# Diagonal-matrix turns, five score banks and earlier value pages in a hybrid decoder step

## The chip, the cores and the metric

One NeuronCore of a Trainium2 chip runs the whole kernel as one program. The metric is the device time of one execution in microseconds; less is better. The engines named below are PE (TensorE; PEld is its weight load), DVE (VectorE), ACT (ScalarE), POOL (GpSimd) and SP (SyncE, which here only issues transfers).

## The reference

One inference step of four layers for a prompt of 1024 tokens and a sample group of 8 sequences with 4 new tokens each, all fp32. Layers 0 and 3 are short convolutions, layer 1 is an RG-LRU block, and layer 2, which the change is about, is differential attention with 8 heads (two score maps of 64 dimensions each, values of 128). The sample's past is 2048 tokens in pages of 128 rows, 16 pages for each sequence, found through a page table.

```python
def diff_combine(p, lam):
    p = p.reshape(p.shape[0], N_HEADS, 2, p.shape[2], p.shape[3])
    return p[:, :, 0] - lam * p[:, :, 1]

# prompt, one block of 128 queries at a time:
sc = jnp.einsum('bqhd,bkhd->bhqk', qi, k)
sc = jnp.where(kpos[None, :] <= qpos[:, None], sc, -jnp.inf)
w = diff_combine(jax.nn.softmax(sc, axis=-1), lam)
o = jnp.einsum('bhqk,bkhd->bqhd', w, v)
# sample: the same over k_past = cache_k[page_table], v_past = cache_v[page_table] and the new rows

def diff_attn_output(o, z, subln_g, lam_init, w_out):
    of = o * lax.rsqrt(jnp.mean(jnp.square(o), axis=-1, keepdims=True) + SUBLN_EPS)
    of = of * subln_g * (1.0 - lam_init)
    return (of.reshape(bsz, t, V_WIDTH) * jax.nn.silu(z)) @ w_out
```

## The kernel before

Tiles are built by Python generators; a scheduler then sets the order on each engine from the order of emission, priorities and its own estimate of times. Layer 2 is `attn_layer`. It runs four main streams one after the other, and lays a side stream into each with `merge(main, total, side, cost)`: every main step yields a number of cost units, and the side stream may spend `cost / total` units for each.

1. `qkv` (line 1099 and around it): queries, keys and values of all tokens, written to DRAM (`qkT`, `vd`). Beside it runs `sample_keys`: POOL issues the 256 half pages of `cache_k` (line 1388 in `page`), DVE transposes each (line 1476), bursts of small matmuls (line 1420) make the scores, then a softmax, and `turn` writes the weights to DRAM (`psd`, lines 1457 and 1458).
2. `zpath`: the gate, 8 heads by 3 chunks of columns, 24 chunks of 24 matmuls (line 127); ACT takes a tanh (line 1160), DVE finishes it (line 1165), and SP stores it to `zd` (line 1166). The tile `zt` has two buffers. The sample keys go on beside it: `shares` of 0.76 and 0.26 divide their cost between the two streams.
3. `heads`: for 8 heads and 8 query blocks each. `keys` and `queries` read a head's keys and queries from DRAM (each 64-row half into both halves of the partitions, by `twice`, line 1183) and split them into a high and a low part. `score` makes the two maps (line 1210) into the banks of `mm`; DVE takes the minimum and adds the mask (lines 1248 and 1250); `expo` takes the exponential on ACT (line 1262). `combine` adds the second map to the first with the factor `rr[:, 10]` on DVE (line 1284). `turn` transposes the sum on PE (line 1293), ACT copies it out (line 1295), `apply` multiplies it with V (line 1303), `finish` scales (line 1312) and squares with a sum (line 1314) on ACT. Three blocks are under way at a time: scores of one, turn and apply of the one before, `finish` of the one before that.
4. Beside the heads runs `sample_values`: SP issues the 128 pages of `cache_v`, 512 KB each, into five buffers (`n_vp`), four matmuls a page accumulate them (line 1524, `sacc`), DVE scales the four row groups out of the bank (line 1530), and `gather_o` transposes them (line 1553).

PSUM has eight banks: tags P (3), Q (1), R (3) and U (1). `deal` says which tags each kind of tile takes in turn. In the heads, scores take R, turns, `pv` and the output's transposes take Q and U, the sample accumulator and `gather_o` take P. While the sample keys run, four of the banks are theirs (`psw`).

SP's queue is in order: a value page that waits for a free buffer holds up whatever SP issues after it.

Of the kernel before, what the change touches and what calls it, by code (L numbers as in the profile page):

```python
# [10 lines left out]
F32 = mybir.dt.float32  # L11
# [35 lines left out]
class Trunk:  # L47
# [31 lines left out]
    def bank(self, kind, name):  # L79
        tag = next(self.deals[kind])  # L80
        pool = self.psb if tag in "PQ" else self.psum
        return pool.tile([128, 512], F32, tag=tag, bufs=self.BANKS[tag], name=name)
# [1061 lines left out]
    def zpath(self, u):  # L1144
        nc, a = self.nc, self.a
        wv = a["d_w_in"][0].rearrange("(k p) f -> p k f", p=128)

        def ld(h):
            c = 3 * D + 128 * h
            return self.load_w(wv[:, :, c : c + 128], f"wz{h}")  # L1150

        wt = ld(0)
        for h in range(KB):
            nxt = ld(h + 1) if h < KB - 1 else None
            for c in range(3):
                c0, n = CH[c]
                npr = min(n, T - c0)
                ps = self.gemm_chunk(wt, u, c, f"zz{h}_{c}")
                t = self.sm(f"zt{h}_{c}")
                nc.scalar.activation(t[:, :n], ps[:, :n], AF.Tanh, scale=0.5)  # L1160
                if npr < n:
                    nc.vector.scalar_tensor_tensor(
                        self.szs[:, h], t[:, npr:n], 1.0, ps[:, npr:n], ALU.add, ALU.mult
                    )
                nc.vector.scalar_tensor_tensor(t[:, :npr], t[:, :npr], 1.0, ps[:, :npr], ALU.add, ALU.mult)  # L1165
                nc.sync.dma_start(self.zd[h][:, c0 : c0 + npr], t[:, :npr])
                yield 10.2 * n
            wt = nxt


    def heads(self, y):
# [13 lines left out]

        def keys(h, g):
# [6 lines left out]
            t = twice(1, h, g)  # L1193
            cs = slice(512 * g, 512 * g + 512)
            nc.scalar.copy(ks[h][:, :, cs], t)
            for s, (own, oth) in enumerate(halves):
                lo = ks[h][oth, s, cs]
                nc.gpsimd.tensor_tensor(lo, t[oth, s], lo.bitcast(F32), ALU.subtract)
# [76 lines left out]
        def combine(x):  # L1275
            qb, P, rr = x["qb"], x["P"], x["rr"]
            N = (qb + 1) * 128
            if N > 512:
# [5 lines left out]
            chain(nc.vector.scalar_tensor_tensor(  # L1284
                P[0][:, :N], P[1][:, :N], rr[:, 10:11], P[0][:, :N], ALU.mult, ALU.add))

        def turn(x):
            h, qb, P = x["h"], x["qb"], x["P"]
            x["w"] = []
            for o, w in chunks(qb):  # L1290
                wp = self.tp(f"wtp{h}_{qb}_{o}")
                for j in range(0, w, 128):
                    nc.tensor.transpose(wp[:, j : j + 128], P[0][:, o + j : o + j + 128], ident)
# [12 lines left out]
        def finish(x):  # L1306
# [7 lines left out]
            nc.scalar.activation(sq, O[0][:, qj], AF.Square, accum_out=ss[0][:, qj : qj + 1])  # L1314
# [16 lines left out]
        for nxt in blocks[1:] + [None, None, None]:  # L1331
# [24 lines left out]
            if old:  # L1356
                turn(old)
                yield 110 * (old["qb"] + 1)
# [36 lines left out]
    def sample_keys(self):  # L1395
# [95 lines left out]
        ck.__exit__(None, None, None)  # L1491
        self.cpb, self.psb = self.pool("psb2", space=PSUM, reuse_waits="tile")

# [55 lines left out]
    def gather_o(self, b, os_):  # L1549
        nc = self.nc  # L1550
        tp = self.tps(f"sot{b}")
# [9 lines left out]
    def attn_layer(self, l, u):  # L1561
# [30 lines left out]
        merge(itertools.islice(z, 20), ztot, keys, self.shares[1] * KEY_COST)  # L1592

        cpa, self.ppa = self.pool("ppa", reuse_waits="tile")
        hs = self.heads(u)
        next(hs)
        merge(z, ztot, keys, self.shares[1] * KEY_COST)
        rest(keys)
        ca, self.pp = self.pool("pp", reuse_waits="tile")
        self.deal(tp="QU", tps="P", mm="R")  # L1600
        tot = 64 * 9 * 110.0 + 288 * 324.0 + 16 * 430
        values = self.sample_values(u)
        next(values)
# [9 lines left out]
        merge(main(), tot, values, VALUE_COST * self.ahead)  # L1613
# [5 lines left out]
    def run(self):  # L1619
# [108 lines left out]
        if self.layers > 2:  # L1728
# [4 lines left out]
            self.shares, self.ahead, self.n_vp = (0.76, 0.26), 1.1, 5  # L1733
# [5 lines left out]
            for cm in (cr, cc, cs):  # L1739
                cm.__exit__(None, None, None)  # L1740
            trunk_bufs()
# [98 lines left out]
```

## Time and profile before

| | us |
|---|---|
| median of 3 runs | 2407.99 |
| lowest, highest | 2405.65, 2415.18 |
| the profiled execution | 2409.33 |
| its span | 2407.7 |

A row of the profile's tables by stage gives, for a window in us from the span's start, each engine's busy time with the number of instructions, the granted TensorE clock as a share of its full speed, the mean busy share of the 16 DMA engines, and what they moved. PE's busy time is modelled from overlapping matmuls, so the time between two starts in the timeline is the better measure of what an instruction costs. A row of waits names who waited, for whom, how long in total, how often, and the longest. The names are the program's tile names: `wtp` the turned P in PSUM, `wt` its copy, `pv` the product with V, `S` scores, `sacc` the sample accumulator, `vp` a value page, `kp` a key page.

### The profile page before, as it was taken

The page shows a single profiled execution, that of the slowest core. Times are in us where ns is not written, and L with a number is a line of the kernel's source. Part 1 is how long each engine was busy: PE and PEld are TensorE (multiplying, and loading weights), DVE is VectorE, ACT ScalarE, POOL GpSimd, SP SyncE. Part 2 cuts the span into 40 slices and gives each one's busy share as a digit, 9 for nine tenths or more (in the row PEclk, how much of TensorE's full clock was granted, in tenths as well). Part 3 has the DMA queues.
Part 4 walks back from the last instruction along what each step waited for, and adds up shares of the span by engine and source line. Part 5 has one row for each costly group of instructions (what it writes and reads, how often), then busy time and mean ns, then how long its engine had stood idle before and what let it go on. Part 6 is the DMA issues. An engine that isn't in the chain of part 4 may idle for free.

```text
span 2407.7 us, 45325 instructions
## 1 busy us (share of the span) xinstructions
PE 2277.3 (95%) x17288; PEld 1946.8 (81%) x17288; DVE 1453.2 (60%) x3015; ACT 929.2 (39%) x1906; POOL 337.1 (14%) x541
## 2 busy tenths in 40 slices
PE   7999999999999999988999998888888999999997
PEld 4989999997888886766666886555557999999997
DVE  6865655457456545656555554677675477666555
ACT  4333333346544423322221113667665243333410
POOL 0200000001001000233223322333220000000000
PEclk9999999999999999999999998999999999999999
DMA  9243344423444535768677766999993222222442
GB/s 329 77 145 111 91 121 150 133 82 120 139 131 124 154 108 171 217 201 255 222 242 253 244 189 203 277 298 291 281 299 116 84 85 62 68 59 70 128 131 76
DMA packets 289391, 393.41 MB, mean 163 GB/s; under 512 B 18749, under 2 KB 197054, under 8 KB 289174
## 3 DMA queue, kind: packets, MB, share of 16 engines
q1 hardware_dynamic: 247190, 306.61, 42.1%
q0 software_dynamic: 20480, 67.13, 9.1%
q10 hardware_dynamic: 21504, 16.78, 2.1%
q8 instruction: 136, 2.23, 0.4%
q14 instruction: 81, 0.66, 0.1%
HBM read 331.14 MB, written 59.31 MB: 162 GB/s over the span
## 4 chain that ended last, share of the span: by engine, by line
PE 64%; issue 13%; DMA 11%; POOLq 5%; POOL 2%; DVE 2%; ACT 1%; SPq 1%; DVEq 0%; ACTq 0%
PE op L127 15%; PE inX L612 12%; PE inZ L612 6%; DMA vp<-cache_v 6%; PE xb L127 4%; PE z L127 4%; POOLq L1381 4%; PE in L127 3%; PE inY L612 3%; PE ada L200 3%; PE in L733 2%; PE in L648 2%; PE g L903 2%; POOL kp L1388 2%; PE sacc L1524 1%
## 5 line engine op out<-in xcount | busy, mean ns | idle before, releaser
L1099 PE MATMUL qk<-wq,ua 128*128 128x512 f32 x1152 | 284.1, 401 | 8.7 <-DVE wq L1067 5.5
L1099 PEld LDWEIGHTS qk<-wq,ua 128*128 128x128 f32 x1152 | 213.2, 189 | 68.4 <-DVE wq L1067 8.1
L1476 DVE STREAM_TRANSPOSE kt<-kp 128x512 f32<-128x512 f32 x256 | 172.0, 697 | 138.5 <-DMA kp<-cache_k 107.1
L1388 POOL DMA_DIRECT2D kp<-cache_k x256 | 137.9, 539 | 336.1 <-DVE kt L1476 188.8
L294 DVE SCALAR_TENSOR_TENSOR r<-op,gate,xr 128x384 f32<-128x384 f32 (+1 forms) x96 | 54.2, 570 | 127.4 <-PE op L127 82.5
L1262 ACT ACTIVATE P<-S,rr 128x512 f32<-128x512 f32 (+2 forms) x192 | 110.8, 583 | 47.1 <-DVE rr L1250 31.5
L1210 PE MATMUL S<-ks,qhl 128*128 128x512 f32 (+2 forms) x384 | 110.8, 395 | 13.8 <-ACT P L1262 7.4
L127 PE MATMUL zz<-ua,wz 128*128 128x384 f32 (+1 forms) x576 | 99.0, 331 | 7.0 <-DVE zt L1165 7.0
L1210 PEld LDWEIGHTS S<-ks,qhl 128*128 128x128 f32 x384 | 60.8, 196 | 54.8 <-ACT P L1262 30.7
L127 PEld LDWEIGHTS zz<-ua,wz 128*128 128x128 f32 x576 | 95.6, 193 | 11.4 <-DVE zt L1165 7.8
L127 PEld LDWEIGHTS z<-ub,wrz 128*128 128x128 f32 x576 | 92.6, 188 | 11.7 <-issue 10.1
L1524 PE MATMUL sacc<-vp,pv 128*16 128x256 f32 x1024 | 80.3, 389 | 22.9 <-DMA vp<-cache_v 22.7
L127 PE MATMUL z<-ub,wrz 128*128 128x384 f32 (+1 forms) x576 | 98.2, 326 | 0.0
L1303 PEld LDWEIGHTS pv<-V,wt 128*128 128x128 f32 x576 | 73.7, 194 | 22.5 <-ACT wt L1295 13.4
L127 PEld LDWEIGHTS xb<-ub,wrx 128*128 128x128 f32 x504 | 80.9, 188 | 12.7 <-issue 9.2
L1420 PE MATMUL sps<-kt,qbd 32*32 32x512 f32 x2048 | 78.8, 621 | 11.9 <-DVE kt L1476 11.9
L331 POOL TENSOR_TENSOR rs<-mv,mhalf 128x1 f32<-128x1 f32 (+1 forms) x36 | 19.1, 541 | 504.3 <-DVE mv L329 497.6
L127 PE MATMUL op<-ua,ub 128*128 128x384 f32 (+1 forms) x504 | 89.7, 333 | 0.0
L127 PEld LDWEIGHTS op<-ua,ub 128*128 128x128 f32 x504 | 81.9, 192 | 9.1 <-issue 9.0
L127 PE MATMUL xb<-ub,wrx 128*128 128x384 f32 (+1 forms) x504 | 87.9, 328 | 0.0
L1303 PE MATMUL pv<-V,wt 128*128 128x128 f32 x576 | 82.3, 284 | 5.8 <-ACT wt L1295 5.3
L200 PE MATMUL ada<-wada,ct 128*32 128x512 f32 x384 | 82.7, 616 | 4.1 <-DMA wada<-w_ada 2.9
(492 smaller groups left out, 5112.4 us busy)
## 6 DMA issues: line engine op xcount, KB each, us to landing
kp<-cache_k POOLq DMA_DIRECT2D x256, 256.0 KB, 3.8
vp<-cache_v SPq DMA_DIRECT2D x128, 512.0 KB, 10.0
wada<-w_ada SPq DMA_DIRECT2D x96, 512.0 KB, 4.2
xa<-xat SPq DMA_DIRECT2D x64, 192.0 KB, 2.6
wra<-a_w_in SPq DMA_DIRECT2D x24, 512.0 KB, 4.1
wrb<-a_w_in SPq DMA_DIRECT2D x24, 512.0 KB, 4.1
xr<-xa SPq DMA_DIRECT2D x64, 192.0 KB, 2.5
tok<-kd SPq DMA_DIRECT2D x32, 256.0 KB, 7.0
```

The costliest lines, as they stand in the source:

```text
L127: nc.tensor.matmul(ps[:, :n], wt[:, wp, k], self.ucols(units[k], up, c), start=i == 0, stop=i == 3 * KB - 1)
L200: nc.tensor.matmul(ps[c : c + 32, :], self.ct[:, k], wts[k // 2][:, k % 2], start=k < 4, stop=k >= 4, tile_position=(0, c),)
L612: nc.tensor.matmul(B[tgt][jj][:, :QH], w[n][:, wp, k], mov[k](jj, up), start=new and m == 0, stop=m == 11, skip_group_check=not new)
L1099: nc.tensor.matmul(ps, u[k][:, c0 : c0 + 128], wq[n, k // 2][:, wp, k % 2], start=i == 0, stop=i == 3 * KB - 1)
L1210: nc.tensor.matmul(st[:, o : o + w], qs[h, g][:, part, s, 128 * qj : 128 * qj + 128], ks[h][:, s, l0 : l0 + w], start=part == 0, stop=part ...
L1262: nc.scalar.activation(p[:, o : o + w], x["S"][s][i][:, :w], AF.Exp, scale=-1.0, bias=rr[:, 6 + s : 7 + s], accum_out=rr[:, c : c + 1])
L1303: nc.tensor.matmul(x["pv"], x["w"][kb // 4][:, j : j + 128], V[h][:, kb], start=kb == 0, stop=kb == qb)
L1381: ld, (r,) = nc.values_load_multi_w_load_instructions(self.ptab[0:1, idx : idx + 1], engines=[et], min_val=0, max_val=159)
L1388: d = eng.dma_start(t, a[src].rearrange(pat)[bass.ds(r, 1), :, cs].rearrange("a p f -> p (a f)"))
L1420: nc.tensor.matmul(ps[b][32 * g : 32 * g + 32, r], qf[rows, f, g, k], kt[rows, g, k], start=f == 0 and k == 0, stop=f == 1 and k == 3, til ...
L1476: nc.vector.transpose(ktv[:, :, j], ring.pop(0).rearrange("p (f t) -> p f t", t=32))
L1524: nc.tensor.matmul(acc[32 * g : 32 * g + 16, :], pt[:k, j, g], vv[:k, :, g], start=j == 0, stop=j == NPG, tile_position=(0, 32 * g))
```

## The change

- `combine` no longer adds the two maps. It makes a 128 x 128 matrix `d` with the factor on its diagonal (DVE). `turn` makes, for each block of 128 columns, two matmuls that accumulate in PSUM: P0 with the identity and P1 with `d`.
- The square and its sum in `finish` move from ACT to DVE.
- PSUM after the sample keys: P has one bank, a new tag V has two. Scores take R, R, R, V, V in turn. `gather_o` takes Q and U in place of P. After layer 2 the pool is opened anew with three P banks.
- `keys` reads each key block once into a [128, 512] tile; ACT copies and POOL subtracts half by half.
- The sample keys must end after 12 of the 24 gate chunks (`shares` 0.8 and 0.4, and `rest(keys)` there). The sample values begin there, at 0.34 of their cost over the whole gate path, and the heads take the rest. `n_vp` is 7.
- In `zpath` the store to `zd` is issued by ACT, one chunk later, behind the next chunk's tanh.
- The pacing of the turns doubles, from 110 to 220 units for each block of 128.

```diff
--- before.py
+++ after.py
@@ -78,7 +78,7 @@
 
     def bank(self, kind, name):
         tag = next(self.deals[kind])
-        pool = self.psb if tag in "PQ" else self.psum
+        pool = self.psb if tag in "PQV" else self.psum
         return pool.tile([128, 512], F32, tag=tag, bufs=self.BANKS[tag], name=name)
 
     def tp(self, name):
@@ -1150,6 +1150,7 @@
             return self.load_w(wv[:, :, c : c + 128], f"wz{h}")
 
         wt = ld(0)
+        late = []
         for h in range(KB):
             nxt = ld(h + 1) if h < KB - 1 else None
             for c in range(3):
@@ -1158,14 +1159,17 @@
                 ps = self.gemm_chunk(wt, u, c, f"zz{h}_{c}")
                 t = self.sm(f"zt{h}_{c}")
                 nc.scalar.activation(t[:, :n], ps[:, :n], AF.Tanh, scale=0.5)
+                if late:
+                    nc.scalar.dma_start(*late.pop())
                 if npr < n:
                     nc.vector.scalar_tensor_tensor(
                         self.szs[:, h], t[:, npr:n], 1.0, ps[:, npr:n], ALU.add, ALU.mult
                     )
                 nc.vector.scalar_tensor_tensor(t[:, :npr], t[:, :npr], 1.0, ps[:, :npr], ALU.add, ALU.mult)
-                nc.sync.dma_start(self.zd[h][:, c0 : c0 + npr], t[:, :npr])
+                late.append((self.zd[h][:, c0 : c0 + npr], t[:, :npr]))
                 yield 10.2 * n
             wt = nxt
+        nc.scalar.dma_start(*late.pop())
 
 
     def heads(self, y):
@@ -1182,6 +1186,7 @@
             for rows in halves[0]:
                 nc.sync.dma_start(t[rows], src.rearrange("(s p) f -> p s f", p=64))
             return t
+
 
         def keys(h, g):
             if g == 0:
@@ -1190,12 +1195,13 @@
                 nc.sync.dma_start(
                     V[h], self.vd[:, 128 * h : 128 * h + 128].rearrange("(j p) f -> p j f", p=128)
                 )
-            t = twice(1, h, g)
+            t = self.raw([128, 512], f"tok1{h}_{g}")
             cs = slice(512 * g, 512 * g + 512)
-            nc.scalar.copy(ks[h][:, :, cs], t)
+            nc.sync.dma_start(t, self.qkT[1][128 * h : 128 * h + 128, cs])
             for s, (own, oth) in enumerate(halves):
-                lo = ks[h][oth, s, cs]
-                nc.gpsimd.tensor_tensor(lo, t[oth, s], lo.bitcast(F32), ALU.subtract)
+                hi = ks[h][own, s, cs]
+                nc.scalar.copy(hi, t[own])
+                nc.gpsimd.tensor_tensor(ks[h][oth, s, cs], t[own], hi.bitcast(F32), ALU.subtract)
 
         def queries(h, g):
             t = twice(0, h, g)
@@ -1273,16 +1279,17 @@
             last.append(inst)
 
         def combine(x):
-            qb, P, rr = x["qb"], x["P"], x["rr"]
-            N = (qb + 1) * 128
-            if N > 512:
+            qb, rr = x["qb"], x["rr"]
+            if qb > 3:
                 chain(nc.vector.tensor_reduce(
                     rr[:, 0:2], rr[:, 16:20].rearrange("p (s i) -> p s i", s=2), axis=AX.X, op=ALU.add))
             chain(nc.vector.reciprocal(rr[:, 4:6], rr[:, 0:2]))
             chain(nc.vector.scalar_tensor_tensor(
                 rr[:, 10:11], rr[:, 0:1], rr[:, 5:6], self.nlam, ALU.mult, ALU.mult))
-            chain(nc.vector.scalar_tensor_tensor(
-                P[0][:, :N], P[1][:, :N], rr[:, 10:11], P[0][:, :N], ALU.mult, ALU.add))
+            x["d"] = d = self.ropep.tile([128, 128], F32, tag="dg", bufs=2, name=f"dg{x['h']}_{qb}")
+            chain(nc.vector.tensor_scalar(d, ident, rr[:, 10:11], None, ALU.mult))
+
+
 
         def turn(x):
             h, qb, P = x["h"], x["qb"], x["P"]
@@ -1290,7 +1297,9 @@
             for o, w in chunks(qb):
                 wp = self.tp(f"wtp{h}_{qb}_{o}")
                 for j in range(0, w, 128):
-                    nc.tensor.transpose(wp[:, j : j + 128], P[0][:, o + j : o + j + 128], ident)
+                    for s, r in enumerate((ident, x["d"])):
+                        nc.tensor.matmul(
+                            wp[:, j : j + 128], P[s][:, o + j : o + j + 128], r, start=s == 0, stop=s == 1)
                 wt = self.pp.tile([128, 512], F32, tag="wt", bufs=self.n_wt, name=f"wt{h}_{qb}_{o}")
                 nc.scalar.copy(wt[:, :w], wp[:, :w])
                 x["w"].append(wt)
@@ -1311,7 +1320,9 @@
                 ss[0] = self.ropep.tile([128, 4], F32, tag="ss", bufs=2, name=f"ss{h}_{g}")
             nc.scalar.activation(O[0][:, qj], x["pv"], AF.Identity, scale=x["rr"][:, 4:5])
             sq = self.ropep.tile([128, 128], F32, tag="sq", bufs=1, name=f"sq{h}_{qb}")
-            nc.scalar.activation(sq, O[0][:, qj], AF.Square, accum_out=ss[0][:, qj : qj + 1])
+            nc.vector.tensor_tensor_reduce(
+                sq, O[0][:, qj], O[0][:, qj], scale=1.0, scalar=0.0, op0=ALU.mult, op1=ALU.add,
+                accum_out=ss[0][:, qj : qj + 1])
 
         def begin(h, qb):
             return dict(h=h, qb=qb, S={}, P=[], rr=self.ropep.tile(
@@ -1355,7 +1366,7 @@
                     out.append((older["h"], older["qb"] // 4, outputs(older["h"], older["qb"] // 4)))
             if old:
                 turn(old)
-                yield 110 * (old["qb"] + 1)
+                yield 220 * (old["qb"] + 1)
                 apply(old)
                 yield 216 * (old["qb"] + 1)
             if cur:
@@ -1489,7 +1500,9 @@
         turn(todo.pop())
         cw.__exit__(None, None, None)
         ck.__exit__(None, None, None)
+        self.BANKS = dict(self.BANKS, P=1, V=2)
         self.cpb, self.psb = self.pool("psb2", space=PSUM, reuse_waits="tile")
+        self.deal(tp="QU", tps="P", mm="RRRVV")
 
 
     def sample_values(self, y):
@@ -1548,7 +1561,7 @@
 
     def gather_o(self, b, os_):
         nc = self.nc
-        tp = self.tps(f"sot{b}")
+        tp = self.tp(f"sot{b}")
         for e in range(2):
             nc.tensor.transpose(tp[:, 128 * e : 128 * e + 128], os_[:, 128 * e : 128 * e + 128], self.ident)
         ov = self.ots[:, :, NQ * b : NQ * b + NQ].rearrange("p (e g) m -> p g e m", e=2)
@@ -1589,18 +1602,18 @@
         cq.__exit__(None, None, None)
         ct, self.tmp = self.pool("tmpq", reuse_waits="tile")
         z, ztot = self.zpath(u), 8 * 10.2 * NT
-        merge(itertools.islice(z, 20), ztot, keys, self.shares[1] * KEY_COST)
-
+        merge(itertools.islice(z, 12), ztot, keys, self.shares[1] * KEY_COST)
+        rest(keys)
+
+        values = self.sample_values(u)
+        next(values)
+        merge(itertools.islice(z, 8), ztot, values, self.zshare * VALUE_COST)
         cpa, self.ppa = self.pool("ppa", reuse_waits="tile")
         hs = self.heads(u)
         next(hs)
-        merge(z, ztot, keys, self.shares[1] * KEY_COST)
-        rest(keys)
+        merge(z, ztot, values, self.zshare * VALUE_COST)
         ca, self.pp = self.pool("pp", reuse_waits="tile")
-        self.deal(tp="QU", tps="P", mm="R")
-        tot = 64 * 9 * 110.0 + 288 * 324.0 + 16 * 430
-        values = self.sample_values(u)
-        next(values)
+        tot = 64 * 9 * 110.0 + 288 * 434.0 + 16 * 430
 
         def main():
             while True:
@@ -1610,7 +1623,7 @@
                     break
                 yield c
 
-        merge(main(), tot, values, VALUE_COST * self.ahead)
+        merge(main(), tot, values, VALUE_COST * (1 - self.zshare / 2) * self.ahead)
         rest(values)
         ca.__exit__(None, None, None)
         cpa.__exit__(None, None, None)
@@ -1730,14 +1743,16 @@
                 cm.__exit__(None, None, None)
             self.bufs = dict(sm=2)
             self.n_sz, self.n_ks, self.n_p, self.n_tok, self.n_wt, self.n_o = 1, 2, 4, 2, 3, 2
-            self.shares, self.ahead, self.n_vp = (0.76, 0.26), 1.1, 5
+            self.shares, self.zshare, self.ahead, self.n_vp = (0.8, 0.4), 0.34, 1.1, 7
             cc, cp = self.pool("acst", reuse_waits="tile", side="right")
             cr, self.ropep = self.pool("ropep", reuse_waits="tile", side="right")
             self.attn_consts(cp)
 
             self.attn_layer(2, A)
-            for cm in (cr, cc, cs):
+            for cm in (cr, cc, cs, self.cpb):
                 cm.__exit__(None, None, None)
+            self.BANKS = dict(self.BANKS, P=3)
+            self.cpb, self.psb = self.pool("psb3", space=PSUM, reuse_waits="tile")
             trunk_bufs()
             ca, self.tmpa = self.pool("tmp1a", reuse_waits="tile")
             cms, B = [ca], []
```

## Rows read from the trace of the kernel before

**Rows 1.** The page's first line.

```profile
span 2407.7 us, 45325 instructions
```

**Rows 2.** Table by stage; columns: window, length, busy of each engine, PEclk, DMA share, GB/s.

```profile
948.00:1350.00 402.00, 375.12 (x3349) 270.37 (x3350) 221.92 (x459) 97.10 (x152) 112.52 (x209) 0.98 0.73 229
1350.00:1418.00 68.00, 61.97 (x636) 55.45 (x636) 40.51 (x79) 13.18 (x23) 20.62 (x39) 0.96 0.75 238
1418.00:1490.00 72.00, 63.03 (x638) 57.27 (x636) 27.40 (x48) 15.98 (x25) 20.59 (x25) 0.94 0.54 154
1490.00:1846.00 356.00, 304.39 (x2464) 200.09 (x2464) 252.52 (x658) 237.03 (x727) 100.53 (x72) 0.97 0.94 270
```

**Rows 3.** Transfers, 1490 to 1846 us: totals, then issues with count, size, median landing.

```profile
DMA packets 41000, 95.99 MB, mean 270 GB/s; under 512 B 3910, under 2 KB 14822, under 8 KB 40960
...
tok<-kd SPq DMA_DIRECT2D x24, 256.0 KB, 7.4
sz<-zd SPq DMA_DIRECT2D x15, 256.0 KB, 7.2
```

**Rows 4.** Groups by line and form, PE, 1490 to 1846: busy, mean ns, idle before.

```profile
L1303 PE MATMUL pv<-V,wt 128*128 128x128 f32 x576 | 82.3, 284 | 5.8 <-ACT wt L1295 5.3 <-ACT O L1312 0.5
L1524 PE MATMUL sacc<-vp,pv 128*16 128x256 f32 x1024 | 80.3, 389 | 22.9 <-DMA vp<-cache_v 22.7
L1210 PE MATMUL S<-ks,qhl 128*128 128x512 f32 x192 | 67.4, 443 | 4.1 <-ACT P L1262 4.0
L1293 PE MATMUL wtp<-ident,P 128*128 128x128 f32 x288 | 46.5, 285 | 8.0 <-DVE P L1284 7.5 <-ACT wt L1295 0.3
L1210 PE MATMUL S<-ks,qhl 128*128 128x256 f32 x124 | 28.4, 324 | 7.8 <-DVE zt L1165 5.9 <-ACT P L1262 1.6
L1210 PE MATMUL S<-ks,qhl 128*128 128x384 f32 x64 | 19.1, 396 | 1.9 <-ACT P L1262 1.8
```

**Rows 5.** Timeline of PE in the heads; columns: start us, length us, group.

```profile
1649.60 0.82 PE L1293 MATMUL wtp<-ident,P 128*128 128x128 f32 x6
1650.34 0.63 PE L1524 MATMUL sacc<-vp,pv 128*16 128x256 f32 x8
1650.90 1.60 PE L1303 MATMUL pv<-V,wt 128*128 128x128 f32 x12
1652.34 0.60 PE L1226 MATMUL ytp<-ident,O 128*128 128x128 f32 x4
...
1657.08 0.96 PE L1210 MATMUL S<-ks,qhl 128*128 128x512 f32 x4
1657.97 0.62 PE L1524 MATMUL sacc<-vp,pv 128*16 128x256 f32 x8
```

**Rows 6.** Waits, 1490 to 1846: engine, line, releaser, total us, times, longest.

```profile
PEld sacc L1524 <- DMA vp<-cache_v: 33.4, 34, 2.3
PEld S L1210 <- ACT P L1262: 30.7, 46, 6.1
...
PEld pv L1303 <- ACT wt L1295: 13.4, 24, 1.3
...
PE wtp L1293 <- DVE P L1284: 7.5, 8, 1.8
```

**Rows 7.** Timeline of POOL, gate path: issues of key pages.

```profile
1446.86 0.54 POOL L1388 DMA_DIRECT2D kp<-cache_k  x1 [0.82 <-issue]
1448.22 0.54 POOL L1388 DMA_DIRECT2D kp<-cache_k  x1 [0.82 <-DVE kt L1476]
```

**Rows 8.** Groups by line, DVE, 1490 to 1846: eviction of the sample accumulator.

```profile
L1530 DVE TENSOR_SCALAR os<-sacc,coef 16x256 f32<-16x256 f32 x32 | 15.4, 480 | 4.1 <-PE sacc L1524 3.6
```

**Rows 9.** Table by stage for 6.8 us of half clock, and PE's timeline there.

```profile
1515.60:1522.40 6.80, 6.18 (x30) 3.31 (x24) 3.06 (x6) 2.46 (x9) 0.00 (x0) 0.50 1.03 308
...
1515.47 1.03 PE L1524 MATMUL sacc<-vp,pv 128*16 128x256 f32 x8 [0.52 <-DMA vp<-cache_v]
```

**Rows 10.** Transfers of line 1166, the gate stores, over the span.

```profile
DMA to landing us min/median/max: 1.7/2.8/4.3
```

## The prediction

> **What bounds the kernel now.** The profiled execution took 2409.3 us, its span 2407.7 us [rows 1]; the median of the three timed runs, 2407.99 us, lies 1.3 us under that execution, and I bring the sum back by that at the end. The first view to read is the table by stage [rows 2]. The change touches four stretches: the projections with the sample keys beside them (948 to 1350 us), the first and second half of the gate path (1350 to 1418 and 1418 to 1490) and the prompt heads with the sample values beside them (1490 to 1846). In the heads no compute engine is full by its own column: PE is busy 304 of 356 us, DVE 253, ACT 237. The DMA share is 0.94, at 270 GB/s. In the second half of the gate path it is only 0.54. The reader should see that the heads hang on transfers, and that the stretch right before them has room for transfers.
>
> The next view, the transfers of the heads [rows 3], says what fills them: 96 MB, of which the 128 value pages of 512 KB (8 batches of 16) are 67 MB. The third view is PE's own work there [rows 4], priced not by busy time (matmuls overlap, and the mean of 284 ns is no pace) but by start to start in the timeline [rows 5]:
> - turning P: 288 instructions; six take 1650.34 - 1649.60 = 0.74 us, 0.123 each, together 36 us.
> - pv: 576 instructions for the 288 products of 128 x 128 (8 heads of 1 + 2 + ... + 8 blocks), so two instructions a product. Twelve take 1652.34 - 1650.90 = 1.44 us, 0.120 each, together 69 us.
> - sacc: eight, one page, take 0.56 us; 136 pages (128 and the 8 new rows, the last left out of the rows shown) make 76 us.
> - scores: four of 512 columns take 0.89 us, 0.2225 each; by columns 192 x 0.2225 + 64 x 0.167 + 124 x 0.111 = 67 us.
> Together 248 us. The other 108 us of the stage are small groups and waiting. The waits that PE's weight loads and matmuls show there [rows 6] are 33.4 us for value pages, 30.7 for score banks (ACT must read one out first), 13.4 for the turned P and 7.5 for the combined P: 85 us. So the stage has 85 us to give, and 23 us that I leave alone.
>
> **The change, part by part.**
> *Turns by a diagonal matrix.* A turn was one PE transpose of P, already combined by DVE. Now every 128 x 128 block takes two true products, P0 by the identity and P1 by the diagonal, added in PSUM. Operands are full fp32 and of the shapes of pv, and pv takes two instructions a product [rows 4]. So 288 instructions become 288 x 2 x 2 = 1152, 864 more. A wait-free pv instruction takes 0.120 us with its share of the change of group [rows 5]; the added ones only make groups longer, so I take somewhat less, 0.1125, an estimate: 864 x 0.1125 = **+97 us** on PE. Bounds: 0.10 to 0.12, so 86 to 104 us. The kernel's own pacing figures double the turn from 110 to 220 ns a block; the rows of pv say 450.
>
> What DVE is spared (the combination of up to 1024 columns, 64 times) and what it is given (a 128 x 128 diagonal and the square with its sum, taken from ACT) lie on engines with 100 us of slack [rows 2]: I cost them at nothing. If DVE were nearly full they would show as waits for the diagonal; the 7.5 us for the combined P fall to about 3, the chain being shorter.
>
> *Five banks for scores.* PE may run two more score tiles ahead of ACT. Of the 30.7 us I leave 9: scores also hang on the softmax's own order, which more banks don't change. Bounds 0 and 25 left.
>
> *Keys read once.* Each key half is read once instead of twice: of the 256 KB reads `tok<-kd` [rows 3] half go, 24 x 0.26 / 2 = 3.1 MB, 11 us of transfer at the stage's 270 GB/s. ACT copies two 64-partition halves instead of one 128-partition tile; hidden.
>
> *Values begin half way through the gate path.* 0.34 x 12/24 = 0.17 of the values' cost is spent there: 0.17 x 8 x 6900 = 9384 units, 400 a page and 500 a batch, about 22 pages. That takes 22 x 0.56 = **12 us** of PE and 11.5 MB out of the heads. The heads then carry 96 - 3.1 - 11.5 = 81 MB, at 270 GB/s 300 us of transfer, well under the PE work; with seven buffers instead of five the 33.4 us for pages fall to about 8 (bounds 2 and 20). The wait for the turned P falls from 13.4 to 9: longer turns hide the first chunk's copy.
>
> Relief in the heads: 85 - (8 + 9 + 9 + 3) = 56 us. **Heads: +97 - 12 - 56 = +29 us.** What is late next is PE itself: 248 + 97 - 12 = 333 us of work in a stage of 385.
>
> *Gate path.* The second half gains the 12 us of sacc; PE was idle there for 72 - 63 = 9 us [rows 2], and I let it absorb 4: +8 (bounds 0 and 14). Keys must now end after 12 chunks: 0.20 x 256 = 51 half pages in that half. POOL issues one every 1448.22 - 1446.86 = 1.36 us at its fastest [rows 7], so 70 us, as long as the whole half (68 us). The score bursts only move (their share of PE before 1350 rises from 0.76 to 0.80 and the gate path loses as much); I add 3 us for waiting on the last pages and the last turn (bounds -5 and +15). The gate stores leave SP, where they would queue ahead of value pages, for ACT's queue, and are issued one chunk later: 24 issues on an engine busy 29 us of 140, cost nothing while they land in time (third rival). **Gate path and keys: +11 us.**
>
> *One bank instead of three for the sample accumulator.* The first sacc of a batch now waits for four evictions of the last, 480 ns each [rows 8], and everything of PE behind it: at most 8 x 1.9 = 15 us, but main work of some microseconds is laid between two batches; I take 0. The pool that swaps these banks back before the last layers costs nothing: it closes when the heads have ended.
>
> Sum: 29 + 11 = +40 us, 2449 us in the profiled execution's terms, **2448 us** as a median.
>
> **A rule against the trace: the clock.** In the heads PE's granted clock averages 0.97; it is at 0.50, 1.2 of 2.4 GHz, from 1515.6 to 1522.4 us among others [rows 9], a stretch of 30 PE instructions whose sacc waits for pages [rows 9]. The Trainium skill, "TensorE: Matmul & The Clock Gate", Part 4 (PE-mode transpose), says that transposes don't count as PE activity for the clock as matmuls do. By it the new turns would hold the clock up by themselves and be worth up to 0.03 x 356 = 10 us, an estimate: 2438 us. The trace puts the drop behind late pages, not behind turns, and I leave the sum.
>
> **The rivals.**
> 1. *Waiting is all that grows less, and all of it goes.* If the whole 85 us vanish and the gate path absorbs its 12, the heads come out at +97 - 12 - 85 = 0 and the total at about 2408 us. For it: more banks, more buffers and a shorter chain all at once. Against: a PE at 333 us of work still has softmax chains between blocks, and PE-bound stretches of this kernel have gaps, as 948 to 1350 with 27 us idle [rows 2]. Chance 0.14, ends 2396 to 2420.
> 2. *The products cost what the pacing says.* If a product with the identity or the diagonal is one instruction like a transpose, the turns add only 288 x 0.1125 = 32 us. The heads then sit on the transfers' 300 us and PE's 268, and the relief outweighs the turns: 32 - 12 - 50 = -30, with +11 for the gate path -19 in all: 2389 us, **faster**. It decides from the instruction count: under about 600 in the turns. Against it: pv has the same types and shape and has two. Chance 0.06.
> 3. *The late store paces the gate path.* A gate tile has two buffers; its store is issued after the next chunk's tanh and must land before the one after that. The chunk can't be shorter than about 0.9 us (tanh and issue) plus the landing. Landing was 1.7 to 4.3 us, median 2.8 [rows 10], and a chunk with its share of pages lasts some 5.2 us, so it decides from a landing of 4.3 us. Beside value pages a read of like size took 7.2 us [rows 3]: 12 x (8.1 - 5.2) = +35, 2483 us. For it: the same wait is there before. Against: ACT's queue is not the pages' queue. Chance 0.13.
>
> **How the numbers follow.** Forecast 0.67 (own range 2420 to 2475), rivals 0.14, 0.06 and 0.13. The bounds of the terms reach from about 2408 (all relief) to about 2488 (25 us of relief, 20 in the gate path). With rival 1 half inside and rival 3 just inside, the range is 2408 to 2484. What a measurement of this kernel can tell from no change is about 0.5%, 12 us, so 2396 to 2420: faster 0.07 (rival 2 and the edge of rival 1), same 0.14 (rival 1 and the forecast's low edge), slower 0.79.
>
> **What would show it.** Turns of 1152 instructions at 0.11 to 0.12 us start to start prove the main term; 576 would prove rival 2. A stage of heads near 385 us with a DMA share near 0.75 and waits for value pages under 15 us would bear out that PE replaced the transfers as the bound; pages still late by 30 us would say that the move of 22 pages was not what they lacked. Waits of ACT for `zd` above 40 us would be rival 3. It goes wrong above all if PE's other waits, which I leave at 29 us, don't behave like a PE-bound stage's.

## The result and the profile after

| | before | changed |
|---|---|---|
| median, us | 2411.31 | 2470.37 |
| lowest, highest | 2405.65, 2415.18 | 2462.66, 2473.45 |
| the profiled execution | 2409.33 | 2470.98 |

The changed kernel takes 1.0242 of the time of before (95% interval 1.0208 to 1.0276): 59 us more. The forecast was 2448, the range 2408 to 2484, the likeliest side "slower". The profiled executions differ by 61.7 us, which I follow here.

Where it lies is read first from two tiles whose first and last matmul bound the heads: the scores `S` begin them, the turned outputs `ytp` end them. The view is that of one tile; columns are count, duration min/median/max in ns, first and last start in us. The kernel before:

```profile
L1210 PE MATMUL S<-ks,qhl x384: 274/392/796, 1482.8 to 1825.8; 128*128 128x512 f32 x96, 128*128 128x256 f32 x64, 128*128 128x384 f32 x32
L1226 PE MATMUL ytp<-ident,O x64: 272/273/421, 1523.4 to 1845.6; 128*128 128x128 f32 x64
```

The changed kernel:

```profile
L1216 PE MATMUL S<-ks,qhl x384: 274/392/505, 1507.4 to 1881.5; 128*128 128x512 f32 x97, 128*128 128x256 f32 x63, 128*128 128x384 f32 x32
L1232 PE MATMUL ytp<-ident,O x64: 270/273/328, 1550.9 to 1907.0; 128*128 128x128 f32 x64
```

The heads begin 1507.4 - 1482.8 = 25 us later and last 1907.0 - 1507.4 = 400 us in place of 1845.6 - 1482.8 = 363: 37 us more. The prediction had +11 and +29.

The table by stage of the changed kernel (columns as in [rows 2]); the heads are cut where the last value page is used:

```profile
948.00:1362.00 414.00, 383.63 (x3365) 272.13 (x3366) 229.12 (x477) 99.43 (x156) 119.87 (x219) 0.96 0.73 229
1362.00:1507.00 145.00, 135.12 (x1398) 109.79 (x1397) 60.53 (x111) 24.97 (x43) 31.58 (x51) 0.95 0.81 261
1507.00:1755.00 248.00, 241.98 (x2157) 172.05 (x2154) 136.26 (x459) 129.05 (x355) 67.64 (x48) 1.00 0.85 282
1755.00:1907.00 152.00, 138.86 (x1033) 126.18 (x1032) 89.13 (x321) 94.22 (x263) 37.10 (x27) 1.00 0.20 58
```

PE is busy 381 of the 400 us of the heads, against 304 of 356 before [rows 2]. The transfers are at 0.85 of their engines until 1755 us and at 0.20 after it. So the stage falls in two: a part with all 108 remaining pages, and 152 us after the last of them, in which PE is still busy 139 us and the transfers have little left.

The groups by line and the waits (columns as in [rows 4] and [rows 6]) for the heads of the changed kernel:

```profile
L1301 PE MATMUL wtp<-ident,P 128*128 128x128 f32 x576 | 113.3, 278 | 0.2 <-ACT O L1321 0.2
L1301 PE MATMUL wtp<-dg,P 128*128 128x128 f32 x576 | 111.5, 275 | 0.0
L1537 PE MATMUL sacc<-vp,pv 128*16 128x256 f32 x868 | 71.0, 383 | 2.8 <-DMA vp<-cache_v 2.8
```

```profile
PEld S L1216 <- ACT P L1268: 27.8, 53, 1.3
...
PE S L1216 <- ACT P L1268: 12.0, 24, 1.1
...
PEld sacc L1537 <- DMA vp<-cache_v: 6.9, 11, 1.4
...
PEld pv L1312 <- ACT wt L1304: 2.2, 7, 0.4
```

The turns are 576 + 576 = 1152 instructions, where there were 288 [rows 4]. No row of waits names the diagonal matrix. The timeline of PE, an unbroken stretch of them:

```profile
1606.44 0.39 PE L1301 MATMUL wtp<-dg,P 128*128 128x128 f32 x2
1606.66 0.39 PE L1301 MATMUL wtp<-ident,P 128*128 128x128 f32 x2
...
1607.78 0.39 PE L1301 MATMUL wtp<-dg,P 128*128 128x128 f32 x2
```

From 1606.44 to 1607.78 us lie 12 instructions: 0.112 us each. 864 more of them are 96 us of PE.

### The profile page after: what moved, and what is told of

Its sections match the earlier page's. It is cut to its first block, busy times and chain, and to the rows that moved or that the text cites. A ratio compares the mean times of both kernels' runs of the same rounds, so it can differ in the third digit from the quotient of the medians.

```text
span 2469.3 us, 47162 instructions
## 1 busy us (share of the span) xinstructions
PE 2372.9 (96%) x18152; PEld 2044.0 (83%) x18152; DVE 1426.7 (58%) x3143; ACT 913.0 (37%) x1794; POOL 340.5 (14%) x541
## 3 DMA queue, kind: packets, MB, share of 16 engines
q1 hardware_dynamic: 241430, 298.22, 37.9%
## 4 chain that ended last, share of the span: by engine, by line
PE 71%; issue 14%; POOLq 5%; DMA 4%; POOL 2%; ACT 1%; DVE 1%; SPq 0%; DVEq 0%; ACTq 0%
PE op L127 15%; PE inX L612 11%; PE inZ L612 6%; PE xb L127 4%; POOLq L1392 4%; PE z L127 4%; PE wtp L1301 4%; PE in L127 3%; PE inY L612 3%; PE sacc L1537 3%; PE ada L200 3%; PE S L1216 3%; PE zz L127 2%; PE in L733 2%; PE pv L1312 2%
## 5 line engine op out<-in xcount | busy, mean ns | idle before, releaser
L1301 PE MATMUL wtp<-ident,P 128*128 128x128 f32 x576 | 113.3, 278 | 0.2 <-ACT O L1321 0.2
L1301 PE MATMUL wtp<-dg,P 128*128 128x128 f32 x576 | 111.5, 275 | 0.0
L1431 PE MATMUL sps<-kt,qbd 32*32 32x512 f32 x2048 | 86.0, 682 | 17.2 <-DVE kt L1487 17.2
L1301 PEld LDWEIGHTS wtp<-ident,P 128*128 128x128 f32 x576 | 88.6, 191 | 9.7 <-issue 4.7
L1216 PEld LDWEIGHTS S<-ks,qhl 128*128 128x128 f32 x384 | 58.8, 189 | 40.0 <-ACT P L1268 27.8
L1301 PEld LDWEIGHTS wtp<-dg,P 128*128 128x128 f32 x576 | 87.4, 192 | 0.4 <-issue 0.4
```

The costliest lines, as they stand in the source:

```text
L1216: nc.tensor.matmul(st[:, o : o + w], qs[h, g][:, part, s, 128 * qj : 128 * qj + 128], ks[h][:, s, l0 : l0 + w], start=part == 0, stop=part ...
L1301: nc.tensor.matmul(wp[:, j : j + 128], P[s][:, o + j : o + j + 128], r, start=s == 0, stop=s == 1)
L1431: nc.tensor.matmul(ps[b][32 * g : 32 * g + 32, r], qf[rows, f, g, k], kt[rows, g, k], start=f == 0 and k == 0, stop=f == 1 and k == 3, til ...
```

## Experiments

Each kernel below was timed in three rounds against the kernel before, on one chip for each group; the kernel before stood at 2410 to 2411 us in all of them. "The changed kernel" stands at 2470.37 us.

### Old turns, all else changed

```diff
-                    for s, r in enumerate((ident, x["d"])):
-                        nc.tensor.matmul(
-                            wp[:, j : j + 128], P[s][:, o + j : o + j + 128], r, start=s == 0, stop=s == 1)
+                    nc.tensor.transpose(wp[:, j : j + 128], P[0][:, o + j : o + j + 128], ident)
```

with `combine` and the pacing as before the change.

> The changed kernel with the old turns: DVE combines the two maps and PE transposes the sum, 288 instructions instead of 1152; pacing as before; all else as changed. Theory (PE's work sets the end of the heads): 864 instructions at 0.112 us, 97 us of PE, go; transfers then limit the stage again at about 81 MB / 0.285 = 285 us, so the heads fall from 400 us to 300 to 325 and the kernel to about 2380 (2370 to 2400). Rival (the turns lie beside other waits and the loss comes from the new order and the moved keys): above 2430.

2381.53 us, 0.9894 of before (0.9869 to 0.9918): the turns cost the changed kernel 89 us, and what is left of the change gains 28 us. The first theory holds in that PE's work sets the end of the heads. The heads by stage:

```profile
1501.00:1816.00 315.00, 289.83 (x2319) 196.28 (x2318) 273.23 (x780) 218.49 (x616) 110.50 (x75) 0.98 0.78 249
```

315 us in place of 400, with PE busy 290 in place of 381. The theory's second half, that transfers limit the stage again, is not shown: the DMA share is 0.78.

### New turns alone

The same edit, the other way round, on the kernel before: the new turns and their pacing alone.

> The kernel before with the diagonal-matrix turns and their pacing alone. Theory: 97 us of PE come in, of which the waits for value pages (33 us) and for the turned and combined P (21 us) can hide some 45: about 2460 (2445 to 2480), value-page waits under 15 us. Rival (transfers stay the bound of the heads and hide the turns): within 12 us of before.

2490.27 us, 1.0347 (1.0309 to 1.0384): 80 us more than before, outside the 2445 to 2480 expected. The theory has the side right, its cover wrong: of the 97 us counted only some 17 were hidden, not 45. The stages, and the wait for pages from 1510 to 1850 us, say why:

```profile
1485.00:1808.00 323.00, 301.52 (x2566) 207.93 (x2568) 149.65 (x455) 166.30 (x493) 80.14 (x58) 0.98 0.93 282
1808.00:1923.00 115.00, 106.23 (x794) 97.38 (x793) 70.20 (x204) 77.41 (x238) 24.91 (x19) 0.99 0.19 55
...
PEld sacc L1525 <- DMA vp<-cache_v: 21.1, 20, 3.8
```

Up to the last page, at 1808 us, the transfers are at 0.93 and pages still come late; then 115 us follow with the transfers at 0.19. The cover that I counted on was there only in the first part, and the pages end long before the stage does.

### One product of the two

```diff
-                    for s, r in enumerate((ident, x["d"])):
-                        nc.tensor.matmul(
-                            wp[:, j : j + 128], P[s][:, o + j : o + j + 128], r, start=s == 0, stop=s == 1)
+                    nc.tensor.matmul(
+                        wp[:, j : j + 128], P[1][:, o + j : o + j + 128], x["d"], start=True, stop=True)
```

> The changed kernel with one of the two products of each turn (P1 by the diagonal; P0 by the identity is left out, so the attention of the first map is missing): 576 instructions fewer. Theory (PE-bound): 576 x 0.112 = 65 us less, 2400 to 2415. Rival (the heads wait for something else as soon as PE has a little room): less than 40 us gained, above 2430.

2398.62 us, 0.9955 (0.9937 to 0.9972): 72 us less than the changed kernel, for 576 instructions, or 0.125 us each. That is the full price of PE's time (0.112 us each) and a little more: the heads of the changed kernel are bound by PE.

### Three score banks, new turns

```diff
-        self.BANKS = dict(self.BANKS, P=1, V=2)
+        self.BANKS = dict(self.BANKS, P=3)
-        self.deal(tp="QU", tps="P", mm="RRRVV")
+        self.deal(tp="QU", tps="P", mm="R")
```

and `gather_o` back on P.

> The changed kernel with the banks dealt as before: three for scores (R), three for the sample accumulator and its transposes (P). The prediction's theory: five banks saved some 20 us of waits for score banks, so 20 us slower, about 2490, with waits of PE's loads for ACT's exponentials of 45 us or more. Rival: these waits (28 us with five banks, 31 with three before) are a fixed cost of each hand-over from ACT and don't hang on the number of banks: within 6 us of the changed kernel.

2469.5 us, 1.0262 (1.0235 to 1.0289), the same as with five. The prediction's relief by banks did not exist here. (The edit also gives the sample accumulator its three banks back, so one bank in place of three costs nothing either, unless the two cancel.) The waits of PE's loads for ACT's exponentials are even smaller with three:

```profile
PEld S L1216 <- ACT P L1268: 20.4, 26, 2.7
```

So the 27.8 us of the changed kernel are no want of banks that costs time; that they are a fixed price of each hand-over, as the rival has it, is not shown by this.

### Values with the heads, new turns

```diff
-            self.shares, self.zshare, self.ahead, self.n_vp = (0.8, 0.4), 0.34, 1.1, 7
+            self.shares, self.zshare, self.ahead, self.n_vp = (0.8, 0.4), 0.0, 1.1, 7
```

> The changed kernel, but no value page is taken before the heads (share of the gate path 0 instead of 0.34). Theory (PE is the bound of the heads, so it does not matter in which stage the pages' 12 us of PE lie): the scores start some 10 us earlier, the heads take some 12 us more: within 10 us of the changed kernel, 2460 to 2480. Rival (early pages save transfer time in the heads): 25 to 40 us slower, about 2500.

2474.38 us, 1.0269 (1.0229 to 1.0309): no difference from the changed kernel. The scores start at 1491.4 us instead of 1507.4, the heads last 419 us instead of 400:

```profile
L1216 PE MATMUL S<-ks,qhl x384: 274/392/505, 1491.4 to 1884.5; 128*128 128x512 f32 x97, 128*128 128x256 f32 x63, 128*128 128x384 f32 x32
L1232 PE MATMUL ytp<-ident,O x64: 270/273/473, 1539.6 to 1910.4; 128*128 128x128 f32 x64
```

What early pages take out of a PE-bound stage they put into the stage ahead.

### Values with the heads, old turns

The same edit on the kernel with old turns.

> The changed kernel with the old turns (2381.5 us) and no value page before the heads. Theory (with the old turns transfers are the bound of the heads again, at 285 to 290 GB/s): 22 pages of 0.524 MB come back, 11.5 MB or 40 us, of which 12 us are given back in the gate path: about 2410 (2398 to 2420). Rival (early values are worth as little as in the PE-bound stage): within 8 us of 2381.

2377.82 us, 0.9864 (0.9827 to 0.9901): not 2410. My theory falls. The early pages are worth nothing here either, and so the heads with old turns are not simply a number of bytes at 285 GB/s:

```profile
1489.00:1813.00 324.00, 302.92 (x2502) 201.48 (x2502) 267.44 (x786) 220.42 (x617) 111.96 (x75) 0.97 0.85 272
```

324 us with some 20 more pages, at a mean of 272 GB/s, only 9 us longer than the 315 without them.

### Keys read twice, old turns

On the kernel with old turns:

```diff
-            t = self.raw([128, 512], f"tok1{h}_{g}")
+            t = twice(1, h, g)
             cs = slice(512 * g, 512 * g + 512)
-            nc.sync.dma_start(t, self.qkT[1][128 * h : 128 * h + 128, cs])
-            for s, (own, oth) in enumerate(halves):
-                hi = ks[h][own, s, cs]
-                nc.scalar.copy(hi, t[own])
-                nc.gpsimd.tensor_tensor(ks[h][oth, s, cs], t[own], hi.bitcast(F32), ALU.subtract)
+            nc.scalar.copy(ks[h][:, :, cs], t)
+            for s, (own, oth) in enumerate(halves):
+                lo = ks[h][oth, s, cs]
+                nc.gpsimd.tensor_tensor(lo, t[oth, s], lo.bitcast(F32), ALU.subtract)
```

> The changed kernel with the old turns and with keys read twice as before. Theory: 13 half reads of 0.26 MB come back in the heads, 3.4 MB or 12 us at 285 GB/s: 2388 to 2395. Rival (the reads fit beside): within 4 us of 2381.

2408.66 us, 0.9994 (0.9976 to 1.0012): 27 us lost, twice what the bytes are worth. The transfers of the heads (SP's queue: packets, MB, share of 16 engines over the window), with keys twice over 1506 to 1839 us, and with keys once over 1501 to 1816:

```profile
q1 hardware_dynamic: 37234, 82.32, 85.3%
```

```profile
q1 hardware_dynamic: 34785, 77.51, 76.7%
```

Keys twice: 0.853 x 333 / 82.32 = 3.45 us of all 16 engines for each MB. Keys once: 0.767 x 315 / 77.51 = 3.12. The doubled reads cost their bytes, and the mean megabyte takes 10% longer; whether the doubled reads themselves are dearer or the transfers beside them is not shown. How it reaches PE is: value pages come late again. PE's loads wait for them, with keys twice and with keys once:

```profile
PEld sacc L1535 <- DMA vp<-cache_v: 22.3, 22, 3.0
```

```profile
PEld sacc L1536 <- DMA vp<-cache_v: 1.2, 5, 0.4
```

### Three score banks, old turns

On the kernel with old turns:

```diff
-        self.BANKS = dict(self.BANKS, P=1, V=2)
+        self.BANKS = dict(self.BANKS, P=3)
-        self.deal(tp="QU", tps="P", mm="RRRVV")
+        self.deal(tp="QU", tps="P", mm="R")
```

and `gather_o` back on P.

> The changed kernel with the old turns and the old banks (three for scores, three for the sample accumulator). Theory after the run with three banks and the new turns: the number of score banks is worth nothing, within 6 us of 2381. Rival (banks do matter once PE is not full): 10 to 25 us slower.

2416.72 us, 1.0031 (1.0012 to 1.0049): 35 us slower than with five banks. The rival holds, beyond its own range. The waits, with three banks and with five:

```profile
PEld S L1216 <- ACT P L1268: 42.0, 62, 2.1
...
PE S L1216 <- ACT P L1268: 19.8, 24, 1.7
```

```profile
PEld S L1216 <- ACT P L1268: 26.0, 46, 2.7
...
PE S L1216 <- ACT P L1268: 10.2, 13, 2.5
```

Where PE has room, more banks turned it into progress here; where PE was full, there was nothing to turn. The 35 us are not the banks' alone: with three banks, old turns and keys read once, but the staging of before, the kernel takes 2392.6 us (keys once alone, below). So with three banks the early values, the seven buffers and the rest of the change lose 24 us, which with five banks they don't (2381.5 here, 2385.0 below). Which of them does it was not run.

### Five banks and keys once on the kernel before

The bank and key parts of the change alone, old turns, five page buffers, all staging as before: the edit of the next section, `gather_o` on Q and U, the pool opened anew after layer 2 as in the change, and

```diff
+        self.BANKS = dict(self.BANKS, P=1, V=2)
+        self.deal(tp="QU", tps="P", mm="RRRVV")
-        self.deal(tp="QU", tps="P", mm="R")
```

> The kernel before with five score banks and keys read once, and nothing else of the change (old turns, keys and values staged as before, five page buffers, gate stores on SP). Theory after the runs with old turns: banks (35 us) and keys read once (27 us) carry the whole gain, the rest of the change costs a little in the stages ahead of the heads: 2360 to 2380, scores starting within 4 us of before. Rival (early values, seven buffers or the late store are needed for it): 2390 or more.

2384.98 us, 0.9896 (0.9862 to 0.9929), in the expected 2360 to 2380 with its lowest run only: 2377.84 to 2390.76. Scores start at 1483.5 us, as before. Most of the gain needs neither the early values nor the late store.

### Keys once alone

```diff
-            t = twice(1, h, g)
-            nc.scalar.copy(ks[h][:, :, cs], t)
+            t = self.raw([128, 512], f"tok1{h}_{g}")
+            nc.sync.dma_start(t, self.qkT[1][128 * h : 128 * h + 128, cs])
```

with the two halves of `ks` made from it as in the change.

> The kernel before with keys read once alone. Theory (a read into 64 partitions keeps the transfer engines longer for each byte, 3.47 us for each MB of all 16 engines in the heads before and 3.12 with keys read once): 331 us of transfer fall to some 290, and as three banks take up part of it, 15 to 30 us faster, 2380 to 2395. Rival (only the bytes count): 3.1 MB, 11 us at most, 2399 to 2409.

2392.6 us, 0.9935 (0.9909 to 0.996): 18 us faster, in the expected range and above what the bytes explain. Transfers over 1490 to 1846 us, the window of [rows 3], with keys once and in the kernel before:

```profile
q1 hardware_dynamic: 43220, 93.67, 83.6%
```

```profile
q1 hardware_dynamic: 40960, 95.51, 93.1%
```

0.836 x 356 / 93.67 = 3.18 us for each MB in place of 0.931 x 356 / 95.51 = 3.47. The loads' wait for value pages falls from 33.4 us [rows 6] to

```profile
PEld sacc L1525 <- DMA vp<-cache_v: 8.2, 9, 2.9
```

with five buffers and no page before the heads. From here the banks are worth another 8 us (2392.6 to 2385.0; the intervals overlap, so this is not settled), less than the 35 us of the run above, where pages also came early and in seven buffers.

### Queries in two transfers of 128 partitions

On the kernel with five banks and keys once:

```diff
-            for rows in halves[0]:
-                nc.sync.dma_start(t[rows], src.rearrange("(s p) f -> p s f", p=64))
+            sv = src.rearrange("(s p) f -> p s f", p=64)
+            for s in range(2):
+                nc.sync.dma_start(t[:, s], sv[:, s].unsqueeze(0).to_broadcast([2, 64, 512]))
```

> The kernel with five score banks and keys read once, and queries read by two transfers into all 128 partitions each (the same bytes as before, which were two transfers into 64 partitions each). Theory (64-partition writes are the slow ones): transfer time in the heads falls below 3.0 us for each MB, 0 to 12 us faster than its base, as transfers are near the end of what binds. Rival (number of partitions plays no part): the same transfer time for each MB and within 4 us of the base.

2507.43 us, 1.041 (1.0378 to 1.0443): 122 us slower than its base, which neither theory had. The heads up to 1700 us of its base, and then its own with the wait for pages:

```profile
1490.00:1700.00 210.00, 192.25 (x1602) 121.57 (x1603) 156.37 (x425) 151.40 (x473) 74.38 (x50) 0.98 1.00 318
```

```profile
1490.00:1700.00 210.00, 144.71 (x1069) 93.12 (x1068) 104.69 (x292) 105.08 (x324) 54.35 (x39) 0.84 0.67 211
...
PEld sacc L1528 <- DMA vp<-cache_v: 76.2, 15, 10.7
...
ACT qhl L1205 <- DMA tok<-qd: 40.4, 8, 8.1
```

(The waits are those of 1490 to 1815 us.) The share of busy transfer engines falls from 1.00 to 0.67 while PE's loads wait 76 us for pages in 15 waits of up to 10.7 us, and ACT waits 40 us for the query tiles themselves. The transfers were held up, not full. The Trainium skill, "DMA: Bandwidth & Descriptors", Rules for kernel authors, says that a leading broadcast dimension of c copies confines a transfer to at most c engines; here c is 2. The trace agrees as far as it goes (the transfer engines are idle for a third of the time), but its rows don't count the engines of one transfer. So this run does not say whether 64 partitions are what makes the doubled reads slow.

### Seven page buffers

On the kernel with five banks and keys once:

```diff
-            self.shares, self.ahead, self.n_vp = (0.76, 0.26), 1.1, 5
+            self.shares, self.ahead, self.n_vp = (0.76, 0.26), 1.1, 7
```

> The kernel with five score banks and keys read once, and seven page buffers instead of five. Theory: with transfers no longer full, two more buffers change the time by less than 5 us against that base. Rival (pages still come late and PE waits): 8 us or more faster.

2377.72 us, 0.9866 (0.984 to 0.989), 7 us under its base, between the two expectations, and the intervals overlap: not settled. With 2374.89 to 2378.55 us it is, beside the kernel with old turns and late values, the fastest of the study: 33 us under before.

## Why the prediction came out as it did

**The main term held.** The turns are 1152 instructions at 0.112 us, as priced from the instruction count of pv [rows 4, 5]; the kernel's own pacing figure of 220 ns a block was wrong by a factor of two, and rival 2 with it. Undoing the turns gives back 89 us, leaving one product out 72. PE took the transfers' place as the bound, as said: busy 381 of 400 us, waits of loads for pages down from 33.4 [rows 6] to 6.9.

**In the heads 8 us were missing, and two terms were off by more than that, in opposite ways.** With the old turns the heads last 315 us in place of 363: the other parts of the change are worth 48 us there, where the prediction had 12 + 56 = 68. The turns, taken last, add 400 - 315 = 85 us, where it had 97. So it is partly luck that the sum came as near as it did.

The term that was off most is that of the score banks, "Of the 30.7 us I leave 9": 27.8 stayed. It read a wait that names ACT's exponentials as a want of banks. With the new turns, three banks take the time of five; with old turns the same edit is worth 35 us in one kernel and 8 us, not clear of noise, in another. So banks can be worth time, but the turns took the room for it away. The other waits came out lower than left over: 6.9 for pages, 2.2 for the turned P, none for the combined P, which is gone, or for the diagonal matrix in its place. That makes 37 us in place of 29, and the prediction's sum with 37 in it gives just the +37 measured; but that is no proof, because the rows of waits are not lost time one by one: PE is idle only 400 - 381 = 19 us, so a part of its loads' waits lies beside running matmuls (the score matmuls themselves wait 12.0 us for the exponentials, the loads 27.8).

The wait for value pages did fall to the 8 us expected, but the seven buffers, to which the prediction gave it, are not needed for that: on the kernel before, reading the keys once brings it to 8.2 us by itself.

**Ahead of the heads 14 us were missing.** I had +3 for the keys and +8 for sacc. The gate path measures 145 us to the first score, against 1482.8 - 1350 = 133 us, so 12; and 20 pages (1024 - 864 weight loads, eight a page) lie in it, of 22 foreseen. The projections end 12 us later, where I had nothing: "the score bursts only move". The last start of the projections' matmuls is 1349.8 us before, 1351.6 to 1353.7 in the other kernels with a share of 0.76 for the keys, and 1355.6 to 1363.5 in all with 0.80. These are single executions, and kernels that differ only in later stages already lie 8 us apart, so the 12 us are rough. Two of these rows, of the fastest kernel and of the changed one:

```profile
L1099 PE MATMUL qk<-wq,ua x1152: 387/396/799, 947.9 to 1351.6; 128*128 128x512 f32 x192
```

```profile
L1099 PE MATMUL qk<-wq,ua x1152: 387/395/792, 948.3 to 1362.0; 128*128 128x512 f32 x192
...
L1084 PE MATMUL qss<-qsp,sel x4: 1057/1140/1221, 1239.9 to 1308.6; 128*128 128x512 f32 x4
...
1239.90:1242.00 2.10, 2.08 (x15) 0.58 (x24) 0.00 (x0) 0.00 (x0) 0.00 (x0) 0.50 0.72 244
```

Part of it shows in the trace: in the changed kernel the sample's row sums at line 1084 run in stretches of half clock (0.50 in the last row), at 1140 ns in place of 592 in the kernel before, and the granted clock over the projections is 0.96 in place of 0.98 [rows 2]. Why the new share leads there is not shown; the share alone was not run.

**Keys read once** were put at 11 us of transfer, hidden. Whether they are hidden in the changed kernel was not run, since the runs on the keys have the old turns. There their size was wrong, since I counted bytes and not how long the engines take for them: 18 us alone and 27 with the other parts.

**Early values** move work from one stage into the other, as said, and change the total by nothing that is clear of noise. They were priced at 12 us. Without them the heads begin 16 us earlier and last 19 us longer with the new turns, 12 earlier and 9 longer with the old. That they bring nothing even with old turns was against my expectation for that run.

**The rivals.** The first asked that all waiting go; 37 us stayed. The third did not occur. The landing of the gate's stores did rise, to a median of 4.8 us, above the 4.3 that I had named, but the chunks lasted 145 / 24 = 6 us, not 5.2, and no tanh waited for a store, whereas in the kernel before ACT waited 37.9 us for them. The row of the waits of before (948 to 1490 us), and the landing in the changed kernel:

```profile
ACT zt L1160 <- DMA zd<-zt: 37.9, 6, 11.5
```

```profile
DMA to landing us min/median/max: 3.0/4.8/6.8
```

The one accumulator bank, put at nothing, costs nothing that shows.

**The clock.** The rule on transposes is neither borne out nor refuted. The granted clock in the heads is 1.00 in the changed kernel and 0.98 with old turns in it, 0.98 with the new turns alone and 0.97 before [rows 2]: in both pairs it is higher with the products. But PE also waits less with them, and the stretch of half clock that costs the kernel with old turns most (0.50 from 1620 to 1626 us) follows a wait:

```profile
1616.90 0.60 PE L1301 MATMUL wtp<-ident,P 128*128 128x128 f32 x4
1620.60 1.09 PE L1301 MATMUL wtp<-ident,P 128*128 128x128 f32 x4 [3.10 <-DVE ots L1569]
```

Transposes stand there too, so the trace does not separate the two. At most 0.02 x 400 = 8 us hang on it, an estimate from these clocks.

**Left open.** The pages end at 1755 us of 1907, so that PE's extra work lies beside transfers at 0.20. Their pacing counts a block's turn at 220 units of a true 450 ns; a right pacing with the new turns was not tried. As PE is idle for only 19 of the 400 us, I would not expect it to win back the 59 us, but that is argued, not shown.

## What to carry to other kernels

Before a cheap-looking PE operation takes work off another engine, count its instructions in the rows of the nearest product of the same types: an fp32 product is two here, a transpose one. A wait that names an engine tells who came last, not which resource is short; the same five banks were worth nothing where PE was full, and 8 us (not clear of noise) and 35 us in two kernels where it was not. Split a bundle of edits: two of this one (banks, keys once) make the kernel 1% faster, and the turns hide them under 89 us.

## What the runs showed of the hardware beyond what I expected

- Reading each key row twice, into 64 partitions each, kept the 16 transfer engines 3.45 to 3.47 us for each MB of the whole stage with the old turns; reading it once into 128 partitions, 3.12 to 3.18. Which property of the doubled reads does it is open.
- Two transfers with a leading broadcast of two copies, for the same bytes, cost 122 us over 16 query tiles: the transfer engines stood at 0.67 of busy while PE waited up to 10.7 us for a value page and ACT up to 8.1 us for a query tile.
